# An order edge that keeps lane work behind the weight split of its k-step

## Chip, cores and metric

One core of one Trainium2 chip. The metric is the device time of one execution in microseconds (us); the median of three runs is quoted. A profile of one further execution shows where the time is. Engines are named as in the profile: PE (TensorE matmul), PEld (its weight loads), DVE (VectorE), ACT (ScalarE), POOL (GpSimd), SP (SyncE, whose queue issues the DMAs).

## What is computed

One layer of a bidirectional hybrid encoder for two requests, a sample of 1024 tokens and a prompt of 256, with shared weights and a width of 2048:

```python
hn = rms_norm(x, norm_g)
proj = hn @ w_in
xbc, z_ssd, dt_raw, q, k, v, z_att, mq, z_mem = split_cols(proj, IN_SIZES)
xbc = silu(centred_dwconv(xbc, conv_w, conv_b))          # 5 taps
y = ssd_scan(forward) + ssd_scan(backward) + d_skip * xs # chunks of 128 tokens, 16 heads
o_ssd = rms_norm(y * silu(z_ssd), ssd_norm_g)            # per group of 512
o_att = window_attention(q, k, v, sink) * silu(z_att)    # |t-s| <= 128, 8 heads
o_mem = softmax(mq @ mk.T) @ mv * silu(z_mem)            # 256 memory tokens, 4 heads
return x + concat([o_ssd, o_att, o_mem]) @ w_out
```

All inputs and outputs are float32.

## The kernel before

The 1280 tokens are ten tiles of 128: tiles 0 to 7 are the sample, 8 and 9 the prompt. They are worked in two groups of five tiles (640 tokens). The transposed activations of a group lie in SBUF as a high and a low part, `xH` and `xL`, both fp32r. A product with a weight is three fp32r matmuls: high by high, high by low, low by high.

**Blocks and k-steps.** The dense products are cut into blocks of output columns. `block_tok` (L245 to L277) has tokens on the partitions: for each of 16 k-steps it loads 128 x 512 raw weights (`wraw`, four buffers, L228), splits them in `wsplit` (L216 to L223) and issues 15 matmuls (L269, L270, L271) into five accumulators `acc`. `block_feat` (L279 to L313) has features on the partitions: eight double k-steps, raw weights from L286, matmuls of 320 columns (L304, L305, L306) into four of the five accumulators. In both, the last two k-steps are done together, so that accumulators finish one after the other, and each is evacuated (`evac`) at once.

**The weight split.** `wsplit` makes the high part on ACT (`wh`, L219, or L222 with a gain) and the low part on DVE (`wl`, L220 or L223). `wh` and `wl` have three buffers each (`WB`), so the split of a k-step can be issued as soon as the matmuls of the k-step three before are through. The splits are traced under `tc.high_priority(offset=100)`.

**Lanes.** Everything else is written as generators that yield between steps, and queued in two lanes (L143 to L175). `run` (L945) goes through a block, and after each k-step calls `pump`, which takes as many lane steps as the block's entry in `RATES` says, from the two lanes in turn. `need` steps a lane until a named piece is done. The pieces that the prediction speaks of:

- `x_stats(t)` (L922): four loads `xst` and squares (L928), a sum (L930), and `rsqrt` on POOL (L133, L134); it gives the norm of token tile t. `mem_stats(i)` does so for the memory (L940).
- `vectors` (L1012): eight small loads (L1017) and the exponential of `aneg` (L1024).
- `mk_prep(i)` and `k_prep(t)`: load, square, sum, `rsqrt` on POOL, scaling, transposes on PE.
- `attn(t)` (L559): a head (load q, square L571, sum L573, `rsqrt`, L577, high and low part L585 and L586, transposes L591 into `pq`), then for four head pairs the scores (L607 to L627), a turn (L637 into `ppt`, L638) and the product with v (L648 into `po`). `mem_attn(t)` is the like for the memory; its head ends in transposes L684 into `pmq`.
- `ssd_up(t)` (L758): one SSD chunk. `weights(q)`, four times a tile, loads `rf` (two buffers) and `rb` (three buffers) from `ac_d` (L840), adds the columns' bias in eight ACT instructions (L848), merges the two directions (L849, DVE), takes the exponential (L850, ACT) and multiplies by `cb` (L851, DVE). `diag(g)` reads the results in the matmuls `py` (L858).
- `ssd_down(t)`: the backward state.

Other buffers of the lanes: tag `wa` has five, shared by x_stats, mem_stats, the preps and the heads of both attentions; `wb` four.

**Who sets the order.** A scheduler places every instruction when the program is built. It goes by priority (the order of tracing, less the offset of `high_priority`), takes an instruction of lower priority where those above it aren't ready in its own model of time, and gives a tile a buffer when one is free. The result is a fixed order for each engine; on the chip an engine takes its instructions in that order, and each waits for its inputs. So lane work whose inputs come from a load alone can stand ahead of splits and evacuations that were traced before it. Evacuations are traced with high priority, too (offset 30 in `block_tok`, 100 in `block_feat`). `tc.issue_after(ins)` adds, for each instruction that its block traces on the engine of `ins`, an edge that puts it behind `ins` in that engine's order; it adds no wait for `ins` to finish. The kernel uses it already for the loads of `x_stats` and `mem_stats` (L927 and L939, behind the last load of the activations).

Of the kernel before, what the change touches and what calls it, by code (L numbers as in the profile page):

```python
# [10 lines left out]
F32 = mybir.dt.float32  # L11
# [4 lines left out]
AF = mybir.ActivationFunctionType  # L16
ALU = mybir.AluOpType
# [23 lines left out]
def hymba_encoder_kernel(  # L41
# [6 lines left out]
    V, A, G, T, S = nc.vector, nc.scalar, nc.gpsimd, nc.tensor, nc.sync  # L48
# [99 lines left out]
    def queue(lane, fn, ts):  # L148
        for t in ts:
            lanes[lane].append(((fn.__name__, t), fn(t)))  # L150

    def step(lane):
        name, gen = lane[0]
        try:
            next(gen)
        except StopIteration:
            lane.popleft()
            done.add(name)

    def pump(n):  # L160
        for _ in range(n):
            turn[0] ^= 1
            lane = lanes[turn[0]] or lanes[turn[0] ^ 1]
            if lane:
                step(lane)

    def need(fn, ts):

        for t in ts:
            while (fn.__name__, t) not in done:  # L170
                step(next(x for x in lanes if any(nm == (fn.__name__, t) for nm, _ in x)))
# [44 lines left out]
    def wsplit(raw, h, l, g=None):  # L216

        if g is None:
            A.activation(h, raw, AF.Copy)  # L219
            V.tensor_sub(l, raw, h.bitcast(F32))  # L220
        else:
            A.activation(h, raw, AF.Copy, scale=g)  # L222
            V.scalar_tensor_tensor(out=l, in0=raw, scalar=g, in1=h.bitcast(F32), op0=ALU.mult, op1=ALU.subtract)  # L223

    def w_laid(src, n, gain=None):

# [18 lines left out]
    def block_tok(w, nt, evac, before_last=None):  # L245
# [4 lines left out]
        for k in range(KT):  # L250
            raw = wp.tile([P, 512], F32, tag="wraw", name="wraw", bufs=RB)
            load(k, raw[:, :n])
            with tc.high_priority(offset=HP[2]):
                h = wp.tile([P, 512], F32R, tag="wh", name="wh", bufs=WB)
                l = wp.tile([P, 512], F32R, tag="wl", name="wl", bufs=WB)
                wsplit(raw[:, :n], h[:, :n], l[:, :n], gcol(k))
            hls[k] = h, l
            if k == KT - 2:
                continue
            if k == KT - 1 and before_last is not None:  # L260
                before_last(k)

            for t in range(nt):
                for k_ in ((k - 1, k) if k == KT - 1 else (k,)):
                    q, m = divmod(k_, 4)
                    h, l = hls[k_]
                    sh = cur["H", q][:, m, t * P:(t + 1) * P]
                    sl = cur["L", q][:, m, t * P:(t + 1) * P]
                    T.matmul(ps[t][:, :n], sh, h[:, :n], start=(k_ == 0), stop=False)  # L269
                    T.matmul(ps[t][:, :n], sh, l[:, :n], start=False, stop=False)  # L270
                    T.matmul(ps[t][:, :n], sl, h[:, :n], start=False, stop=(k_ == KT - 1))  # L271
                if k == KT - 1:
                    with tc.high_priority(offset=HP[0]):
                        evac(t, ps[t])
            if k == KT - 1:
                yield k - 1
            yield k  # L277

    def block_feat(name, evac):  # L279
# [4 lines left out]
        for kk in range(KT // 2):  # L284
            raw = wp.tile([P, 512], F32, tag="wraw", name="wraw", bufs=RB)
            S.dma_start(raw, src[kk])  # L286
            with tc.high_priority(offset=HP[2]):
                h = wp.tile([P, 2, 256], F32R, tag="wh", name="wh", bufs=WB)
                l = wp.tile([P, 2, 256], F32R, tag="wl", name="wl", bufs=WB)
                wsplit(raw, h.rearrange("p a c -> p (a c)"), l.rearrange("p a c -> p (a c)"))  # L290
            hls[kk] = h, l
            if kk == KT // 2 - 2:
                continue
            tail = kk == KT // 2 - 1

            for kks in ([(kk - 1, kk)] if tail else [(kk,)]):
                for f in range(2):
                    for k in [2 * x + j for x in kks for j in range(2)]:
                        q, m = divmod(k, 4)
                        sh, sl = [x[:, k % 2, f * P:(f + 1) * P] for x in hls[k // 2]]  # L300
                        for half in range(2):
                            c = slice(half * 320, half * 320 + 320)
                            o = ps[f][half][:, :320]
                            T.matmul(o, sh, cur["H", q][:, m, c], start=(k == 0), stop=False)  # L304
                            T.matmul(o, sh, cur["L", q][:, m, c], start=False, stop=False)  # L305
                            T.matmul(o, sl, cur["H", q][:, m, c], start=False, stop=(k == KT - 1))  # L306
                    if tail and f == 0:
                        with tc.high_priority(offset=HP[1]):
                            evac(0, ps[0])
            for k in range(2 * kks[0], 2 * kk + 2):  # L310
                yield k
# [247 lines left out]
    def attn(t):  # L559
# [93 lines left out]
        for step in range(6):  # L653
            if step < 4:
                scores(step)
                yield
            if step >= 2:
                values(step - 2)
                yield
            if 1 <= step <= 4:  # L660
                turn_(step - 1)
                yield
# [517 lines left out]
```

## Time and profile before

| | |
|---|---|
| median of 3 runs | 1917.64 us (1916.83 to 1919.4) |
| profiled execution | 1925.01 us; its span, first to last instruction, 1923.3 us |
| mean granted TensorE clock | 0.994 |
| ACT L219, wh, 128x512, 384 times | 626 ns each |
| DVE L220, wl, 128x512, 384 times | 688 ns each |
| PE L269, 128x512, 1408 times | 406 ns each, pipelined |
| ACT L848, rf and rb, 160 times each | 390 and 391 ns each |
| DVE L849, 40 times | 757 ns each |
| load of rf, of rb (256 KB) | 3.8 and 4.2 us from issue to landing (median) |
| DMA | 289.40 MB, mean 150 GB/s |

How to read the views: a line of the waits gives the engine and line that waited, what released it, the sum in us, the number of times and the longest. A line of the timeline gives the start and length in us, engine, source line, instruction, output and inputs, and in brackets the idle time of the engine before it and what ended it. A line of the stages gives from and to, then the busy time and instructions of PE, PEld, DVE, ACT and POOL, the granted clock, the DMA share and GB/s. Matmuls are pipelined: each is shown with its whole length, and the next one starts before it ends.

### The profile page before, as it was taken

Reading aid. Unit: us, or ns where it says so; the run is one execution under the profiler, and the core shown is the slowest. Engines: PE = TensorE matmul, PEld = TensorE weight load, DVE = VectorE, ACT = ScalarE, POOL = GpSimd, SP = SyncE. Lnnn points to the kernel's source line nnn. Section 1 sums busy time; section 2 is a strip of 40 time slices with the busy share of each in tenths; the row PEclk is TensorE's granted clock in tenths of the full one; section 3 lists DMA queues with packets and bytes.
Section 4 is the critical chain, followed back from the end, with each engine's and each line's share of the span. In section 5 each row is a group of like instructions: output and inputs, shape, how many; then the busy total and the mean of one; then the engine's idle time right before and its main releaser. Section 6 shows DMA issues by size and latency. Waiting matters only on the chain.

```text
span 1923.3 us, 28675 instructions
## 1 busy us (share of the span) xinstructions
PE 1875.9 (98%) x10568; PEld 1634.2 (85%) x10568; DVE 1049.4 (55%) x2133; ACT 760.9 (40%) x1721; POOL 81.6 (4%) x147
## 2 busy tenths in 40 slices
PE   8999989999999999999999999999999999999999
PEld 6779989998898879999978778978978787778887
DVE  4443646677564555667776554576675454542222
ACT  6462463333452545423436444334453333421121
POOL 1010010000000000000100000000000000000000
PEclk9999999999999999999999999999999999999999
DMA  8683563233343545433444567655555345454432
GB/s 272 198 257 104 157 182 121 85 114 109 116 124 113 154 140 172 138 96 101 140 131 142 158 177 247 209 187 162 170 158 186 123 149 159 136 176 132 133 120 69
DMA packets 191340, 289.40 MB, mean 150 GB/s; under 512 B 18977, under 2 KB 68193, under 8 KB 191201
## 3 DMA queue, kind: packets, MB, share of 16 engines
q1 hardware_dynamic: 191056, 287.53, 48.9%
q8 instruction: 83, 1.36, 0.3%
q14 instruction: 57, 0.46, 0.1%
q10 hardware_dynamic: 144, 0.06, 0.0%
HBM read 230.59 MB, written 56.92 MB: 149 GB/s over the span
## 4 chain that ended last, share of the span: by engine, by line
PE 77%; DMA 11%; ACT 4%; DVE 4%; issue 2%; POOL 1%; SPq 1%; ACTq 0%; DVEq 0%; POOLq 0%
PE acc L269 14%; PE acc L270 14%; PE acc L271 14%; PE acc L304 8%; PE acc L305 8%; PE acc L306 8%; DMA xst<-in_x_sample_dram 2%; DMA rf<-ac 2%; PE po L648 2%; PE py L858 1%; PE ppt L637 1%; DMA rb<-ac 1%; DVE wl L220 1%; PE pst L826 1%; PE pst L817 1%
## 5 line engine op out<-in xcount | busy, mean ns | idle before, releaser
L269 PE MATMUL acc<-wh,xH 128*128 128x512 f32 (+1 forms) x1568 | 619.0, 395 | 9.0 <-ACT wh L219 5.6
L270 PE MATMUL acc<-wl,xH 128*128 128x512 f32 (+1 forms) x1568 | 601.6, 384 | 2.9 <-DVE wl L220 2.7
L271 PE MATMUL acc<-wh,xL 128*128 128x512 f32 (+1 forms) x1568 | 600.3, 383 | 0.0
L220 DVE TENSOR_TENSOR wl<-wraw,wh 128x512 fp32r<-128x512 f32 (+1 forms) x416 | 278.3, 670 | 384.4 <-ACT wh L219 376.1
L219 ACT ACTIVATE wh<-wraw 128x512 fp32r<-128x512 f32 (+1 forms) x416 | 254.1, 612 | 528.7 <-PE acc L271 268.0
L304 PE MATMUL acc<-xH,wh 128*128 128x320 f32 x1280 | 406.1, 317 | 9.0 <-DVE zs L331 4.7
L306 PE MATMUL acc<-xH,wl 128*128 128x320 f32 x1280 | 396.6, 310 | 1.6 <-DVE wl L220 1.4
L305 PE MATMUL acc<-xL,wh 128*128 128x320 f32 x1280 | 396.6, 310 | 0.0
L269 PEld LDWEIGHTS acc<-wh,xH 128*128 128x128 f32 x1568 | 296.4, 189 | 69.2 <-issue 8.4
L270 PEld LDWEIGHTS acc<-wl,xH 128*128 128x128 f32 x1568 | 296.7, 189 | 62.9 <-issue 6.6
L271 PEld LDWEIGHTS acc<-wh,xL 128*128 128x128 f32 x1568 | 296.2, 189 | 56.5 <-issue 0.6
L304 PEld LDWEIGHTS acc<-xH,wh 128*128 128x128 f32 x1280 | 241.3, 189 | 15.0 <-DVE zs L331 5.2
L305 PEld LDWEIGHTS acc<-xL,wh 128*128 128x128 f32 x1280 | 241.3, 189 | 3.3 <-issue 3.2
L306 PEld LDWEIGHTS acc<-xH,wl 128*128 128x128 f32 x1280 | 241.1, 188 | 2.3 <-DVE wl L220 2.3
L223 DVE SCALAR_TENSOR_TENSOR wl<-wraw,vec,wh 128x512 fp32r<-128x512 f32 x64 | 48.0, 750 | 128.0 <-ACT wh L222 128.0
L222 ACT ACTIVATE wh<-wraw,vec 128x512 fp32r<-128x512 f32 x64 | 46.3, 723 | 145.4 <-PE acc L271 132.3
L379 DVE SCALAR_TENSOR_TENSOR c<-u,vec,c 128x638 f32<-128x638 f32 (+1 forms) x96 | 84.5, 880 | 1.0
L848 ACT ACTIVATE rb<-rb,wj_all 128x128 f32<-128x128 f32 x160 | 53.0, 391 | 49.1 <-DMA rb<-ac 46.5
L848 ACT ACTIVATE rf<-rf,wj_all 128x128 f32<-128x128 f32 x160 | 53.6, 390 | 33.5 <-DMA rf<-ac 33.5
L622 ACT ACTIVATE lg<-lg,nm 128x384 f32<-128x384 f32 (+1 forms) x80 | 45.1, 564 | 46.2 <-DVE nm L616 46.1
L849 DVE COPY_PREDICATED rb<-upper,rf 128x512 f32<-128x512 uint32 x40 | 30.3, 757 | 53.0 <-ACT rb L848 52.8
L214 DVE SCALAR_TENSOR_TENSOR xL<-chd,vec,xH 128x640 fp32r<-128x640 f32 (+1 forms) x48 | 39.6, 837 | 23.5 <-ACT xH L213 23.5
(238 smaller groups left out, 1725.5 us busy)
## 6 DMA issues: line engine op xcount, KB each, us to landing
wraw<-in_w_in_laid_dram SPq DMA_DIRECT2D x288, 256.0 KB, 2.8
wraw<-in_w_out_laid_dram SPq DMA_DIRECT2D x128, 256.0 KB, 2.7
chd<-in_x_turned_dram SPq DMA_DIRECT2D x32, 320.0 KB, 4.1
rf<-ac SPq DMA_DIRECT2D x40, 256.0 KB, 3.8
rb<-ac SPq DMA_DIRECT2D x40, 256.0 KB, 4.2
out_dram<-yt SPq DMA_DIRECT2D x40, 256.0 KB, 3.6
wraw<-in_w_mem_laid_dram SPq DMA_DIRECT2D x32, 256.0 KB, 4.3
xst<-in_x_sample_dram SPq DMA_DIRECT2D x32, 256.0 KB, 4.9
```

What stands on the lines that cost most here:

```text
L219: A.activation(h, raw, AF.Copy)
L220: V.tensor_sub(l, raw, h.bitcast(F32))
L222: A.activation(h, raw, AF.Copy, scale=g)
L223: V.scalar_tensor_tensor(out=l, in0=raw, scalar=g, in1=h.bitcast(F32), op0=ALU.mult, op1=ALU.subtract)
L269: T.matmul(ps[t][:, :n], sh, h[:, :n], start=(k_ == 0), stop=False)
L270: T.matmul(ps[t][:, :n], sh, l[:, :n], start=False, stop=False)
L271: T.matmul(ps[t][:, :n], sl, h[:, :n], start=False, stop=(k_ == KT - 1))
L304: T.matmul(o, sh, cur["H", q][:, m, c], start=(k == 0), stop=False)
L305: T.matmul(o, sh, cur["L", q][:, m, c], start=False, stop=False)
L306: T.matmul(o, sl, cur["H", q][:, m, c], start=False, stop=(k == KT - 1))
L379: V.scalar_tensor_tensor(out=c[:, :n], in0=u[:, k:k + n], scalar=cw[k], in1=c[:, :n], op0=ALU.mult, op1=ALU.add)
L848: A.activation(r[:, c], r[:, c], AF.Identity, bias=wj_all[:, t, h:h + 1])
```

## The change

`wsplit` keeps its two instructions in a list, `marks`, which always holds those of the last split traced. `step` now takes a lane step inside one `issue_after` for each of them. With that, every ACT instruction of the step stands behind the ACT half of the last traced split in ACT's order, and every DVE instruction behind the DVE half in DVE's order. That split is the one of the k-step after which the step is pumped (in the last two k-steps of a block, the block's last). Instructions of PE, POOL and SP, the loads among them, get no edge. The evacuations, the refills of the activations and `x_rows(1)`, which is not taken through `step`, get none.

```diff
+    marks = []
+
     def step(lane):
         name, gen = lane[0]
         try:
-            next(gen)
+
+            with ExitStack() as st:
+                for ins in marks:
+                    st.enter_context(tc.issue_after(ins))
+                next(gen)
         except StopIteration:
             lane.popleft()
             done.add(name)
...
         if g is None:
-            A.activation(h, raw, AF.Copy)
-            V.tensor_sub(l, raw, h.bitcast(F32))
+            a = A.activation(h, raw, AF.Copy)
+            b = V.tensor_sub(l, raw, h.bitcast(F32))
         else:
-            A.activation(h, raw, AF.Copy, scale=g)
-            V.scalar_tensor_tensor(out=l, in0=raw, scalar=g, in1=h.bitcast(F32), op0=ALU.mult, op1=ALU.subtract)
+            a = A.activation(h, raw, AF.Copy, scale=g)
+            b = V.scalar_tensor_tensor(out=l, in0=raw, scalar=g, in1=h.bitcast(F32), op0=ALU.mult,
+                                       op1=ALU.subtract)
+        marks[:] = a.ins, b.ins
```

## The prediction

> **What bounds the kernel now.** I read the busy shares first, then the start times of PE's matmuls, then what DVE and ACT did ahead of each PE gap, and last the clock.
>
> From the page's first part:
>
> ```profile
> PE 1875.9 (98%) x10568; PEld 1634.2 (85%) x10568; DVE 1049.4 (55%) x2133; ACT 760.9 (40%) x1721; POOL 81.6 (4%) x147
> ```
>
> PE is busy all the time, DVE and ACT about half. In an undisturbed stretch the 512-column matmuls start every 0.227 us and the 320-column ones every 0.147 us, so I laid every PE start in the timeline against that pace. Gaps of over 0.45 us beyond it: 28, together 41.2 us. That is nearly all that an order of instructions can win. It can lose more.
>
> The largest gap is at a block's end. Timeline of DVE (start, length, instruction, idle before it):
>
> ```profile
> 253.70 0.88 DVE L331 TENSOR_TENSOR zs<-acc,rbc 128x320 f32<-128x320 f32 x2
> 256.72 0.73 DVE L849 COPY_PREDICATED rb<-upper,rf 128x512 f32<-128x512 uint32 x1 [2.14 <-ACT rb L848]
> 258.36 0.69 DVE L220 TENSOR_TENSOR wl<-wraw,wh 128x512 fp32r<-128x512 f32 x1
> 259.94 0.29 DVE L471 TENSOR_TENSOR kr<-kr,krr 128x128 f32<-128x128 f32 x1 [0.89 <-POOL krr L134]
> 260.15 0.88 DVE L331 TENSOR_TENSOR zs<-acc,rbc 128x320 f32<-128x320 f32 x2
> ```
>
> and of PE:
>
> ```profile
> 260.69 0.63 PE L304 MATMUL acc<-xH,wh 128*128 128x320 f32 x1 [4.43 <-DVE zs L331]
> ```
>
> PE waits for the second L331, which frees an accumulator. Ahead of it in DVE's queue stand L849 of `ssd_up(0)`, whose result PE reads at 516, and L471 of `k_prep(3)`; both sit out their inputs, and all behind them waits. ACT does the same on lane loads:
>
> ```profile
> ACT rb L848 <- DMA rb<-ac: 46.5, 23, 4.8
> ACT rf L848 <- DMA rf<-ac: 33.5, 23, 4.3
> ACT xst L928 <- DMA xst<-in_x_sample_dram: 15.6, 13, 3.8
> ```
>
> A gap costs more than its length. Stages of the span (PE busy, then the others, the clock, the DMA share):
>
> ```profile
> 57.94:64.77 6.83, 6.14 (x14) 4.81 (x15) 1.98 (x3) 2.75 (x5) 0.00 (x0) 0.50 0.62 189
> 64.77:71.60 6.83, 6.83 (x32) 5.64 (x30) 1.68 (x3) 2.43 (x4) 0.00 (x0) 1.00 0.28 84
> 259.33:266.15 6.82, 5.46 (x22) 5.42 (x23) 4.15 (x11) 4.85 (x14) 0.58 (x1) 0.50 0.81 257
> 1402.79:1406.20 3.41, 3.41 (x14) 2.82 (x14) 2.13 (x5) 0.60 (x1) 0.00 (x0) 0.50 0.91 320
> 1631.48:1634.90 3.42, 3.42 (x10) 2.65 (x9) 0.69 (x1) 0.57 (x1) 0.00 (x0) 0.50 0.79 268
> ```
>
> The granted clock is 0.50 for 6.8 us after the gaps of 3.54 (at 58.6) and 4.60 us (at 260.7), and for 3.4 us after those of 1.54 (at 1401.2) and 2.80 us (at 1630.8). Against the usual pace that lost a further 3.0, 2.4, 1.6 and 1.6 us.
>
> **The change, part by part.** It adds no instruction. The edge goes to ACT's and DVE's work of a step; the step's DMAs (SP) and its `rsqrt` (POOL) get none.
>
> *What moves.* I followed the source's queues and numbered each step with the split it is issued with, then laid that beside the order in which ACT and DVE ran. Today 408 of 861 lane operations on ACT (178 us of work) and 197 of 1148 on DVE (109 us) run ahead of that split. 315 and 93 of them are `ssd_up`'s, its weights (L848 to L850) by 9 to 332 us; the rest is `x_stats`, `k_prep`, `mk_prep` and `attn`'s head. The others trail their split already, mostly by three splits, because PE hands them their input.
>
> *What it removes.* Gaps that a moved operation made, clock loss included:
> - 254 to 266: 0.45 + 4.60 + 2.4 = 7.5 us. `ssd_up` and `k_prep(3)` go; `x_stats(6)` belongs to splits issued just there and may stay. I take 6.
> - 137 to 148: 0.62 + 1.20 + 1.15 = 3.0. DVE's splits stood behind `mk_prep`, which waits 1.4 us for POOL three times; it belongs to splits of 167 and later. I take 3.
> - 285 and 295: 0.61 + 1.98, by `attn(0)`'s head and `x_stats(8, 9)`, due at 320 to 340. I take 2.6.
> - 935 and 1511: 1.08 + 1.67, by `k_prep(6, 7)` and `attn(9)`'s head. I take 2.5.
> - 58.6: 3.5 + 3.0. ACT sat 5.0 us before `vectors`' aneg L1024 with an evacuation L411 behind it; but that evacuation also needed the store mq<-mkr, which SP issued at 53.3 behind eight small loads (L1017) and which landed at 57.9. Those loads don't move. Ends 0 and 6.5, I take 2.
> - 771, 1146, 1192, 1216, 1389, 1401, 1423: 10.9 us, where moved weights on ACT or DVE were one cause of several. Ends 0 and 10.9, I take 4.
>
> Sum 20; at most 33.
>
> *What it adds.* A lane operation now waits behind a split, and that waits for PE to free wh: up to 5.5 us at a time (ACT wh L219 on PE acc L271, 268 us in all). Queued behind it on ACT are other lane work and evacuations; behind those DVE, and PE's next lane step. For `ssd_up`'s weights I cost that at nothing: eight L848 of 0.39, L849 0.76, L850 0.63, L851 0.68 make some 5.2 us with the overlap of starts, and from today's split to the first py L858 that reads them there are 13.0 us (tile 6) to 44 us. The cover is two or three k-steps of matmuls (15 x 0.227 = 3.4 us each). Without it each py waits as at 1171 (1.10 us). For the rest I pushed every moved operation to its split and on along its data: no PE instruction came late; the nearest have 5.3 us left (`mk_prep`), 9.4 (`attn`), 9.6 (`k_prep`).
>
> *Buffers.* Loads keep their early start but hold their buffers (rf 2, rb 3, wa 5) until the split. In the densest place, tile 5, the splits of the first and third weights end at 1058.0 and 1062.3: rf is free at about 1062.5, reloaded (3.8 us) by 1066.5, and the weights done by 1072; py reads them at 1084.7. SP waits in order for that buffer, and raw weights stand behind; four raw buffers cover it.
>
> *New gaps.* The moved work takes its waits for POOL and neighbours along. Today it costs PE about 16 us (the first four points); at the new places 0 if the loads have long landed and no evacuation stands behind, 16 if it is as bad there. I take 8, the middle, since the loads' waits go and the POOL waits stay.
>
> Net: 8 - 20 = -12 us. The profiled execution took 1925.0 us (span 1923.3), 7.4 more than the median of 1917.6; it would take 1913, and the median 1906.
>
> **Two rules weighed.** Row: the clock halved after gaps of 1.54 and 2.80 us. The Trainium skill (TensorE: Matmul & The Clock Gate, "HAM oscillation") puts the limit at idle of some 3.4 us; this trace does not bear that limit out. By the page the 1.6 us of clock in the last point would be no gain, and the net an estimated -11.
>
> Row: at 1630.8 PE waited for `mem_attn(8)`'s head, which doesn't run early today. The Trainium skill (Perfetto Trace Analysis, "Optimization Strategy") advises to make what the busy engine waits for start sooner. By that advice an edge that starts lane work later is a step the wrong way; the third case below prices this from rows.
>
> **The rivals.**
> 1. *Given back:* evacuations now meet the same lane work at other block ends, new gaps of 16 to 24 us. For it: 287 us of work only changes its place. Against: its loads will have landed. Time 1914 to 1921.
> 2. *No effect:* the order hardly changes. Against it: 605 operations must move. I count it into the first.
> 3. *Slower:* heads of attention tiles (load, L571, L573, POOL 1.65 us, L577, L585) lose their lead, and PE stands at the transposes. The price is in the timeline of PE:
>
> ```profile
> 1630.79 0.63 PE L684 MATMUL pmq<-ident,mq 128*128 128x128 f32 x4 [2.64 <-issue]
> ```
>
> 2.8 us and 1.6 of clock, 4.4 a head; it decides from five heads on (22 against 20). Eight of the ten `attn` heads would give 35 - 20 = +15, so 1933. For it: `mem_attn(8, 9)`, with no lead, do wait. Against: there three steps lay within about one k-step; `attn`'s heads keep 9.4 us.
>
> **How the numbers follow.** Forecast 0.63, given back 0.11, slower 0.26. A change of 0.2% (3.8 us) is about what a measurement of this kernel can tell. Predicted is 1906. Low end: all 33 us gained less 8, 1893. High end: just short of the third case, 1931. The forecast's own range is 1893 to 1913.
>
> **What would show it.** Right: no gap at 255 to 261 and 137 to 148, L848 of `ssd_up(0)` no earlier than about 480, ACT's waits for rf, rb and xst loads down from 107 us to under 70, PE gaps of over 0.45 us nearer 25 than 41 us. Wrong: gaps of PE at pq L591, ppt L637 or py L858, or more half-clock stages than these four.

## The result and the profile after

The kernel after takes 1896.99 us (median of 4 runs, 1895.86 to 1898.42), beside 1918.52 us for the kernel before on the same chip (4 runs, 1916.83 to 1923.84): ratio 0.9871, 95% interval 0.985 to 0.9891. That is 21.5 us less; forecast were 12 less. The profiled executions are 1925.01 and 1896.01 us, 29.0 apart, so some 7 us of that difference belong to the one execution before and not to the kernels. A second profile of the kernel before (below) has its gaps in the same places and somewhat shorter.

All of the difference lies between PE's matmuls. Laid against the usual pace as in the prediction, PE's starts are late by 55.3 us in all before and by 26.4 after, 28.9 less. Gaps of over 0.45 us went from 28 (41.2 us) to 15 (18.3 us); half-clock time from 20.5 us in four stages to 10.2 in two.

The first part of the page after, busy times by engine:

```profile
PE 1868.3 (99%) x10568; PEld 1631.4 (86%) x10568; DVE 1053.4 (56%) x2133; ACT 758.3 (40%) x1721; POOL 80.6 (4%) x147
```

The counts are those of before: nothing was added, only placed differently. (Lines behind the edit are numbered 6 to 8 higher than before: the split is L225 and L226, the 512-column matmul L277, the accumulator's L331 is L339, the weights L848 to L851 are L856 to L859, py is L866.)

DVE's timeline after, at the block's end where before it stood idle 2.14 us for ACT's rb and 0.89 for POOL's krr, with L331 behind them:

```profile
240.21 0.83 DVE L341 SCALAR_TENSOR_TENSOR zs<-th,zs 128x640 f32<-128x640 f32 x1 [0.81 <-ACT th L340]
241.24 0.69 DVE L226 TENSOR_TENSOR wl<-wraw,wh 128x512 fp32r<-128x512 f32 x1 [0.20 <-ACT wh L225]
241.99 0.93 DVE L339 TENSOR_TENSOR zs<-acc,rbc 128x320 f32<-128x320 f32 x2
243.00 0.69 DVE L226 TENSOR_TENSOR wl<-wraw,wh 128x512 fp32r<-128x512 f32 x1
...
248.56 0.29 DVE L479 TENSOR_TENSOR kr<-kr,krr 128x128 f32<-128x128 f32 x1 [1.08 <-POOL krr L134]
```

Both L339 now run in one go between two splits, with no lane work ahead of them, and PE has no gap there. The wait for POOL is no shorter (1.08 us, before 0.89), but it falls at 248.6, after the evacuation, and PE has no gap there either. `ssd_up(0)`'s first L856 starts at 463.1, where before it was 237.7.

ACT's waits for its lane loads (releaser, sum in us, times, longest), which came to 46.5, 33.5 and 15.6 on these lines before:

```profile
ACT rb L856 <- DMA rb<-ac: 24.3, 8, 5.3
ACT xst L936 <- DMA xst<-in_x_sample_dram: 10.2, 8, 3.9
ACT rf L856 <- DMA rf<-ac: 2.0, 3, 1.0
```

What PE waits for after:

```profile
PE acc L277 <- ACT wh L225: 5.4, 1, 5.4
PE pr L202 <- DVE ch L199: 4.0, 4, 1.5
PE pmq L692 <- issue: 3.4, 2, 2.2
PE ppt L645 <- DVE lg L635: 2.6, 2, 1.4
PE acc L277 <- DVE zs L329: 1.8, 1, 1.8
PE pcb L783 <- DMA bc<-xbc_d: 1.4, 1, 1.4
```

The first is the start of the kernel (5.4 us until the first split). Of the two waits at `ppt`, the longer one falls at 377 and is new. DVE's timeline ahead of it:

```profile
375.28 0.75 DVE L585 SCALAR_TENSOR_TENSOR q<-q,rx,qr 128x512 f32<-128x512 f32 x1 [1.77 <-POOL qr L134]
...
376.62 0.61 DVE L635 TENSOR_SCALAR lg<-lg,den 128x256 f32<-128x256 f32 x2
```

L585 belongs to the head of the next attention tile. It waits 1.77 us for POOL ahead of L635, the last step before the transposes for which PE stands.

Evacuations behind lane work (`zs L331`, 4.7 us before) have left the list but for `zs L329`, a new one. Its place in DVE's timeline:

```profile
1092.60 0.68 DVE L859 TENSOR_TENSOR rb<-rb,cb 128x512 f32<-128x512 f32 x1
1093.96 0.69 DVE L329 SCALAR_TENSOR_TENSOR zs<-th,acc 128x512 f32<-128x512 f32 x1 [0.69 <-DMA z<-zs]
...
1096.77 0.69 DVE L329 SCALAR_TENSOR_TENSOR zs<-th,acc 128x512 f32<-128x512 f32 x1 [1.52 <-DMA z<-zs]
```

The evacuation L329 waits for the store of an earlier zs to give back its buffer, in a stretch where tile 5's weights are now made (L859). That store took 4.58 us from issue to landing (1092.10 to 1096.68), right behind a load of `rf` that SP issued at 1091.54. With the edge on all steps but `ssd_up`'s (below), no such load stands there, the same store was issued at 1092.03 and landed after 2.69 us, and PE has no gap. PE loses 2.01 us here, and the clock halves behind it (stages: PE, PEld, DVE, ACT, POOL busy, granted clock, DMA share, GB/s):

```profile
1091.50:1098.33 6.83, 4.91 (x21) 3.42 (x20) 4.62 (x9) 4.68 (x10) 0.00 (x0) 1.00 0.65 213
1098.33:1105.16 6.83, 6.83 (x26) 6.06 (x25) 2.82 (x5) 1.56 (x4) 0.00 (x0) 0.50 0.71 218
1603.50:1606.92 3.42, 3.42 (x12) 2.75 (x11) 0.67 (x1) 0.50 (x1) 0.00 (x0) 0.50 0.83 288
```

The second stage costs a further 3.3 us against the pace. The third follows the 2.38 us that PE stands at `mem_attn(8)`'s head (`pmq L692 <- issue` above), which stood there before too (2.80).

### The profile page after: what moved, and what is told of

It is laid out like the page before. It is cut to its first block, busy times and chain, and to the rows that moved or that the text cites. A ratio compares the mean times of both kernels' runs of the same rounds, so it can differ in the third digit from the quotient of the medians.

```text
span 1893.9 us, 28656 instructions
## 1 busy us (share of the span) xinstructions
PE 1868.3 (99%) x10568; PEld 1631.4 (86%) x10568; DVE 1053.4 (56%) x2133; ACT 758.3 (40%) x1721; POOL 80.6 (4%) x147
## 4 chain that ended last, share of the span: by engine, by line
PE 92%; DMA 4%; DVE 1%; ACT 1%; issue 1%; POOL 0%; SPq 0%; ACTq 0%; DVEq 0%
PE acc L277 17%; PE acc L278 17%; PE acc L279 17%; PE acc L312 10%; PE acc L314 10%; PE acc L313 10%; PE po L656 2%; PE py L866 2%; PE ppt L645 1%; PE pmo L743 1%; PE pyb L914 1%; PE pyf L820 1%; DMA ch<-o 1%; PE psc L615 1%; PE pst L825 1%
## 5 line engine op out<-in xcount | busy, mean ns | idle before, releaser
L277 PE MATMUL acc<-wh,xH 128*128 128x512 f32 (+1 forms) x1568 | 618.0, 394 | 7.6 <-ACT wh L225 5.4
L226 DVE TENSOR_TENSOR wl<-wraw,wh 128x512 fp32r<-128x512 f32 (+1 forms) x416 | 278.5, 670 | 398.5 <-ACT wh L225 359.9
L225 ACT ACTIVATE wh<-wraw 128x512 fp32r<-128x512 f32 (+1 forms) x416 | 255.3, 614 | 599.2 <-PE acc L279 286.3
L277 PEld LDWEIGHTS acc<-wh,xH 128*128 128x128 f32 x1568 | 295.6, 189 | 68.2 <-issue 8.0
L856 ACT ACTIVATE rb<-rb,wj_all 128x128 f32<-128x128 f32 x160 | 52.9, 390 | 24.3 <-DMA rb<-ac 24.3
L856 ACT ACTIVATE rf<-rf,wj_all 128x128 f32<-128x128 f32 x160 | 51.6, 390 | 2.0 <-DMA rf<-ac 2.0
L219 ACT ACTIVATE xH<-chd,vec 128x640 fp32r<-128x640 f32 (+1 forms) x48 | 37.3, 790 | 30.5 <-DMA chd<-in_x_turned_dram 10.1
```

Of the source, the lines that this page charges most:

```text
L225: a = A.activation(h, raw, AF.Copy)
L226: b = V.tensor_sub(l, raw, h.bitcast(F32))
L856: A.activation(r[:, c], r[:, c], AF.Identity, bias=wj_all[:, t, h:h + 1])
```

## Experiments

Three theories went in. **Theory 1**: each gap is made by particular lane work that stands ahead of an evacuation or a split, and goes when that work stands behind. **Theory 2**: splits get ahead of lane work in general, so that the gain goes with the number of operations held back. **Theory 3**: any new order of the queues shifts gaps, and this one fell well by luck. Every ratio is to the kernel before, run beside it on the same chip (its medians: 1913.51 us for the first four experiments, 1911.68 for the next four, 1916.8 for the last four).

### Only `ssd_up`'s steps get the edge

```diff
-                for ins in marks:
+                for ins in marks if name[0] == 'ssd_up' else ():
```

> The edges are kept for the steps of ssd_up alone (315 of the 408 ACT and 93 of the 197 DVE operations that the change moves). Theory 1 (each PE gap was made by particular lane work that stood, with its inputs not yet there, ahead of an evacuation or a split; removing that work removes that gap): the gap at 260 (4.6 us and its clock loss) loses its longest cause, L849, and shrinks to 0 to 2.5 us, the gaps from 771 to 1423 go (about 9 of 10.9 us), while 58.6, 137 to 148, 285, 295, 935 and 1511 stay (15.8 us with clock); time 10 to 14 us under before, ratio about 0.994. Theory 2 (the splits themselves come sooner, whatever lane work is moved; ssd_up has two thirds of it): two thirds of the 21.5 us, so 14 us, with the gaps thinned everywhere alike. Theory 3 (any new order falls a per cent up or down, the gaps have no one cause): no relation of gaps to the work moved, time anywhere from -25 to +15 us.

1906.26 us, ratio 0.9962 (0.9949 to 0.9976): 7.3 us less, under what was expected. 22 gaps with 27.3 us stay. What PE waits for:

```profile
PE acc L277 <- ACT mkr L419: 3.3, 1, 3.3
PE acc L312 <- DVE u L371: 2.7, 1, 2.7
PE acc L278 <- DVE wl L226: 2.3, 4, 1.0
PE acc L312 <- DVE zs L339: 1.8, 1, 1.8
```

`zs L339`, the 260 gap, is 1.8 us instead of 4.4: `ssd_up(0)` has gone from ahead of it, `k_prep(3)` and `x_stats(6)` have not. The gap at 58, the pair at 140 and 145 and the one at 289 stay.

### All steps but `ssd_up`'s get it

```diff
-                for ins in marks:
+                for ins in marks if name[0] != 'ssd_up' else ():
```

> The edges are kept for all lane steps but ssd_up's. Theory 1: the gaps at 58.6, 137 to 148, 285, 295, 935 and 1511 go (15.8 us with clock), that at 260 stays in part (L849 still stands there), those from 771 to 1423 stay; time 13 to 18 us under before, ratio about 0.992; the gains of this run and of the one with ssd_up alone add up to the whole, 21.5 us. Theory 2: a third of the whole, 7 us. Theory 3: anywhere, and the two don't add up.

1892.62 us, ratio 0.9887 (0.9871 to 0.9903): 20.9 us less, about the whole change's effect. All of the early gaps are gone but for 0.53 us at 54 and 0.69 at 245, and there is none near 1097. Of those from 771 to 1423, which were expected to stay, several are there (1.96 at 1122, 1.31 at 1375). Its waits:

```profile
ACT rb L856 <- DMA rb<-ac: 44.9, 25, 5.1
ACT rf L856 <- DMA rf<-ac: 31.2, 24, 7.3
```

ACT still waits 76 us for `ssd_up`'s loads, as before the change, and the kernel is fast. So those waits cost little once the other lane work is held back, and theory 2 falls: 408 of the 605 operations that had run ahead of their split are `ssd_up`'s, and holding them alone gave 7.3 us; holding the other 197 gave 20.9. Theory 1 had expected the two parts to add up, and they do not: 28.2 is more than the whole's 21.5. Both parts take a share of the 260 gap, and `ssd_up`'s edges bring the new gap at 1097 (it is at 1110, 1.54 us, with them alone).

### Only ACT's edge, only DVE's

```diff
-        marks[:] = a.ins, b.ins
+        marks[:] = a.ins,
```

> Edges for the lanes' ACT operations alone. Most moved DVE operations read what a moved ACT operation writes and would follow by data, but the scheduler places them by its own clock. Theory 1: all but the gaps made by DVE work with no ACT ahead of it goes; 17 to 21.5 us under before. Theory 2: the ACT half of the split comes first in its chain, so as much as the whole change. Theory 3: anywhere.

1893.54 us, ratio 0.989 (0.9874 to 0.9906): 20.0 us less.

```diff
-        marks[:] = a.ins, b.ins
+        marks[:] = b.ins,
```

> Edges for the lanes' DVE operations alone; ACT may run lane work ahead as before, and sits before loads (xst, mkr, aneg, rf, rb) as before, about 100 us in sum. Theory 1: DVE's queue is clear at 255 to 260 (L849 and L471 no longer ahead of L331) and at 137 to 148, so those 10 us go; ACT's share stays (58.6, 295 and part of the rest); 8 to 14 us under before. Theory 2: little, since the ACT half of each split is still late; 0 to 6 us. Theory 3: anywhere.

1900.02 us, ratio 0.9925 (0.9912 to 0.9939): 13.5 us less. The gap at 57 is the one early gap that DVE's edge leaves, at 2.27 us and with 3.4 us of half clock; those of 137 to 148 and 255 to 261 are gone under either edge. Lane steps go from ACT to DVE and back, so that holding one half holds much of the other. The traces show it. Take the longest sequence that two kernels' orders share and count what falls out of it: against the kernel before, that is 283 of DVE's 2133 instructions with both edges and 244 with ACT's alone, 394 of ACT's 1721 with both and 240 with DVE's alone. The intervals of ACT's edge alone and of the whole change overlap.

### The edge goes to the split of two k-steps earlier

```diff
+    hist = []
...
-        marks[:] = a.ins, b.ins
+        hist.append((a.ins, b.ins))
+        marks[:] = hist[max(0, len(hist) - 3)]
```

> The changed kernel with looser edges: a lane step stands behind the split two k-steps before its own. Of the moved operations nearly all ran three splits or more ahead, so they still move. Theory 1 (the gaps were made by lane work far ahead of its place with inputs not there): as the changed kernel within 0.4%, 18 to 24 us under before, and the gaps at 58, 137 to 148, 255 to 261, 285, 295 gone. Theory 2 (it is the splits' being first that pays): a part is lost, since splits can again stand behind lane work of two k-steps; 8 to 16 us under before. Theory 3 (any new order falls a per cent up or down): anywhere, with other gaps.

1892.23 us, ratio 0.9892 (0.9871 to 0.9913): 19.4 us less. A looser edge does as well. The lane work only must not run ahead by a whole block; how closely it follows the split decides nothing. 15 gaps with 18.7 us, as in the kernel after, at partly other places (1.37 at 56, 1.15 at 452, 1.52 at 1481; none at 1097).

### A control: another order without edges

The kernel before, with the weight splits traced at a priority offset of 90 instead of 100:

```diff
-HP = (30, 100, 100)
+HP = (30, 100, 90)
```

> A control: the kernel before, with no edges, and the splits' priority offset 90 in place of 100, which makes the scheduler place the program anew but leaves lane work free to run ahead. Theory 1: lane work still stands ahead (ssd_up's first L848 near 238 us), gaps of over 0.45 us keep a sum of 30 to 50 us, time within 8 us of before. Theory 2: the splits come a little later, 0 to 6 us over before. Theory 3: a change of 10 to 25 us up or down, as large as that of the change.

1915.02 us, ratio 1.001 (0.9996 to 1.0024). What PE waits for:

```profile
PE acc L304 <- DVE zs L331: 5.5, 1, 5.5
PE acc L269 <- ACT mkr L411: 3.2, 1, 3.2
PE acc L306 <- DVE wl L220: 2.2, 2, 1.6
```

The large gaps are those of the kernel before: 5.61 at 260, 3.31 at 59, the group from 137 to 146; one of 1.77 at 427 is new. As a test of theory 3 this is weak, since the order is nearly the old one: by the same count only 25 of ACT's instructions and 84 of DVE's left it, where the change moved 394 and 283. More weighs that `ssd_up`'s edges alone moved 320 and 188 and left the gaps of the other lane work standing, while four ways of holding that work back lost the same gaps.

### Only `vectors` gets the edge

```diff
-                for ins in marks:
+                for ins in marks if name[0] == 'vectors' else ():
```

> Edges for the steps of vectors alone (one ACT and three DVE operations). It asks what made the gap at 58.6 (3.5 us, with 3.0 of clock). If it was ACT sitting before aneg: the gap is gone. If it was the store mq<-mkr, which SP issued behind the small loads (which keep their place): a gap of 2 to 3.5 us stays near 58. All other gaps as before.

1910.38 us (one execution). PE's waits:

```profile
PE acc L312 <- DVE zs L339: 4.7, 1, 4.7
PE acc L277 <- ACT mkr L419: 1.9, 1, 1.9
```

The gap at 56 stays at 2.09 us with aneg out of the way, so aneg was not its main cause. In the kernel after, ACT's timeline has the evacuation itself waiting for the store, the wait that PE shares no longer:

```profile
53.07 0.60 ACT L419 ACTIVATE mkr<-acc 128x512 f32<-128x512 f32 x1 [3.73 <-DMA mq<-mkr]
```

SP issued that store at 49.2, before at 53.3, in both cases behind five of the eight small loads (of the others one is issued at 16, two at 70 or later): 43.8 to 48.0 after, 48.0 to 52.7 before, where one of them held SP for 2.05 us instead of 0.33. Some other step's ACT edge must have drawn these loads forward: the gap is gone or under 0.6 us with the edge on ACT alone and with the edge on all but `ssd_up`, and stays with the edge on DVE alone.

The traces point to `mem_stats`. In the kernel before, its squares stand ahead of splits and wait for their loads:

```profile
42.52 0.63 ACT L940 ACTIVATE mst<-mst 128x512 f32<-128x512 f32 x1 [1.91 <-DMA mst<-in_mem_prompt_dram]
49.34 0.63 ACT L940 ACTIVATE mst<-mst 128x512 f32<-128x512 f32 x1 [1.92 <-DMA mst<-in_mem_prompt_dram]
```

Between 30 and 52 us ACT waits 5.9 to 6.4 us for these loads of the prompt's memory in each of the six profiles with a gap of 2.09 to 3.54 us, 3.2 us in the experiment with the split of two k-steps earlier, where the gap is 1.37, and not at all in the seven others, where it is under 1 us. A raw weight load of SP stands until 44.5 for the split behind the first of these squares, and the small loads and the store follow it. An edge for `mem_stats` alone was not tried.

### The heads of the last two memory tiles first

With the kernel after, 2.4 and 1.4 us of gap stay at pmq, where `mem_attn(8)` and `mem_attn(9)` come right behind `mem_swap`. Here the first step of each (load of mq, its norm) is queued ahead of `mem_swap`; all edges are kept:

```diff
-    queue(0, mem_swap, [0])
-    queue(0, mem_attn, range(8, 10))
+    late = {t: mem_attn(t) for t in (8, 9)}
+
+    def heads(_):
+        for t in (8, 9):
+            next(late[t])
+            yield
+
+    queue(0, heads, [0])
+    queue(0, mem_swap, [0])
+    for t in (8, 9):
+        lanes[0].append((("mem_attn", t), late[t]))
```

> The changed kernel, with the first step (load, square, sum, norm, scale) of mem_attn(8) and mem_attn(9) queued before mem_swap, where it stood behind it and behind mem_attn(8). After the change PE still waits 2.4 and 1.4 us at their transposes (L692, at 1602 and 1623), with 1.6 us of halved clock after the first. Theory 1: both gaps and the half-clock stage go, 3 to 5.4 us under the changed kernel. Against it: the next wait in the same chain (the refill of the last activations behind mem_attn(9), 1.6 and 1.2 us at 1653 and 1674) takes it back; 0 to 2 us.

1886.71 us, ratio 0.9862 (0.9839 to 0.9885). Both pmq gaps are gone.

### The best ones side by side

The kernel after, that with the heads first, the same with the edge for all but `ssd_up`, and the kernel before once more with a profile:

> The changed kernel once more, beside the next two on one chip. Ratio to before 0.985 to 0.990; the gap at 1097 (2.0 us) with its half-clock stage, and those at 1602 and 1623, are there again.

> The changed kernel with the heads of mem_attn(8) and mem_attn(9) queued before mem_swap, beside the changed kernel on one chip. Theory 1: the two gaps and the half-clock stage (5.4 us) are gone from its end, so 3 to 6 us under the changed kernel. Against it: 0 to 2 us, if the refill of the last activations waits the longer.

> The heads queued before mem_swap, and edges for all lane steps but ssd_up's. With edges for the rest alone no gap showed near 1097 (2.0 us and 3.0 of clock in the changed kernel, where an evacuation waits with its store behind pinned weights), but 1.6 us at 1122 and 1.3 at 1375 stayed. Theory 1: the two about cancel, within 3 us of the run with the heads alone. If the edges for ssd_up were worth what they are worth alone (7 us): 7 us slower than that run.

> The kernel before once more, for a second profile: the executions of it on this chip lay between 1908 and 1920 us, the first profiled one at 1925. Theory 1: the gaps at 58, 137 to 148, 255 to 261, 285 to 295 and 1400 to 1423 are there in both, and the difference is in their lengths and in the number of half-clock stages. Theory 3: the gaps are elsewhere.

After: 1894.59 us, ratio 0.9887 (0.9872 to 0.9902). Heads first: 1884.37 us, ratio 0.9837 (0.9822 to 0.9852), 10.2 us under the kernel after and the fastest of all. Heads first without `ssd_up`'s edges: 1888.91 us, ratio 0.9862 (0.9847 to 0.9876); that is 4.5 us more, between the 3 and the 7 us of its expectation. The intervals of the two ratios just overlap, but the five executions of the one (1883.38 to 1887.66) all lie below the four of the other (1888.44 to 1892.14). With the heads first, `ssd_up`'s edges thus seem worth having; without, the two kernels were not told apart (0.9871 and 0.9887, on different chips). The kernel before: 1914.39 us.

Stages of the kernel after, then of the one with heads first, over the places of pmq and of the transposes pr that follow:

```profile
1597.60:1604.00 6.40, 5.60 (x25) 4.77 (x26) 2.39 (x4) 1.23 (x2) 0.00 (x0) 0.73 0.86 285
1649.00:1657.00 8.00, 6.65 (x21) 5.30 (x22) 3.81 (x8) 1.19 (x2) 0.00 (x0) 0.57 0.49 159
```

```profile
1590.00:1597.00 7.00, 7.00 (x34) 5.83 (x33) 4.39 (x8) 3.07 (x6) 1.21 (x2) 1.00 0.92 276
1640.00:1648.00 8.00, 7.59 (x41) 6.06 (x41) 6.10 (x12) 3.70 (x7) 0.00 (x0) 1.00 0.65 186
```

The expectation of 3 to 6 us counted the two pmq gaps (3.8 us) and a stage of clock. Between the two profiles lie 12.0 us: 3.8 at pmq, 2.7 at pr (the gaps there went from 4.2 to 1.5 us), and most of the other 5.5, as far as can be argued, is 13.7 us of half clock that the second one lacks.

PE's waits in the second profile of the kernel before:

```profile
PE acc L304 <- DVE zs L331: 4.7, 1, 4.7
PE acc L269 <- ACT mkr L411: 2.4, 1, 2.4
```

Its gaps stand where they stood in the first one (2.55 at 57, the pair at 139 and 144, 4.83 at 257, 1.98 at 291), 34.8 us in all beside 41.2, and PE's starts are 45.0 us late beside 55.3. The gaps belong to the order, their exact lengths to the execution. Against this profile the kernel after has 18.6 us less, against the first 28.9; the 21.5 of the medians lie between.

## Why the prediction was right, and where it was off

The forecast, faster because the gaps that lane work makes are lost, came out; the measured time lies in its own range (1893 to 1913), 9 us below its value. The terms it took for gains, 20 us in all, came to 30.6 against the first profile of the kernel before (7.5, 3.0, 2.6, 2.75, 6.5 and 8.3) and to some 22.5 against the second, where the same gaps are shorter (7.0, 2.3, 2.0, 2.2, 4.1 and 4.9). By its own steps:

- **The bound.** Right: the gain is in PE's gaps, 28.9 of 29.0 us between the profiles.
- **254 to 266, 137 to 148, 285 and 295, 935 and 1511**: taken 6, 3, 2.6 and 2.5 us. All went, whole. Reserving 1.5 us for `x_stats(6)` was wrong; it made no gap. That the first has two causes is shown: with `ssd_up` alone held back the 260 gap is 1.9 us, with only the other steps held back it is gone, 0.69 being left at 245.
- **58.6**: taken 2 between ends of 0 and 6.5; it was the whole (6.5, and 4.1 by the second profile). This term was mis-sized the most: it held SP's loads for fixed, because they get no edge (and counted eight ahead of the store, where there are five). They did not move in SP's order past the store, but the whole group ran some 4 us sooner, and the store with it; the traces point to `mem_stats`, which the term did not have. An edge on one engine moved when another engine's queue got through.
- **771 to 1423**: taken 4 of 10.9; 8.3 went (0.78, 1.31 and 0.54 stay; 4.9 by the second profile). Too small as well: moved work that was named as one cause of several was mostly the one that decided.
- **Outside the list**: some 5 us more by the first profile (0.98 at 470, 1.56 at 668, about 1 of the 2.57 at 984, several of half a microsecond or less), 2 to 3 by the second. The sum had nothing for them; their causes were not tried.
- **New gaps**: taken 8, the middle of 0 and 16. Measured: 1.39 at 377, 0.63 at 961, 0.55 more at 1002, 2.01 and 3.3 us of clock at 1097, together 7.9. That the sizes agree is luck. The reason given, waits for POOL that go along, holds for 1.39 us: L585 at 377, ahead of L635; the wait at 248.6 cost PE nothing. Two thirds came from a store's buffer at 1097, in `ssd_up`'s dense tile 5, which the term did not have; and at 1002 a wait of ACT for a load of `rb`, ahead of attention's exponentials, was not lost but grew (4.76 to 5.32 us).
- **`ssd_up`'s weights at nothing**: right at the reader. PE's waits at py do not grow (gaps of 0.83 and 0.54 beside 1.10 and 1.54). The price fell on the evacuation's buffer instead, at 1097.
- **The third case, heads losing their lead**: PE has no wait at pq. The `ppt L645 <- DVE lg L635` at 377, 1.39 us in each kernel with edges on `attn` and absent without them, is not of this kind: the head that waits for POOL there is done 9.4 us before its own transposes. Nearest to it is the 0.63 us at 961, where `k_prep`'s transposes L492 wait for `kh` L484. It needed five heads at 4.4 us.
- **The clock rule.** The Trainium skill (TensorE: Matmul & The Clock Gate, "HAM oscillation") puts the limit at some 3.4 us of idle. The runs bear out the row rather than the page: half clock came after gaps of 1.49 (heads first, at 1097) and 2.01 us (after, at 1097). To count the clock as a gain was right for the large gaps; for a gap of 1.5 us it is a matter of the execution, as the last section shows.
- **The advice to start sooner** (the Trainium skill, Perfetto Trace Analysis, "Optimization Strategy") was weighed as speaking against this change. For the heads at pmq it holds (10.2 us with the gaps behind them). Against the change it did not speak: what PE waited for at 260 was the evacuation, and that starts sooner because `k_prep` and `ssd_up` start later.
- **Signs.** Gaps at 255 to 261 and 137 to 148 gone, 463 for the first weight of `ssd_up(0)` where 480 was named as the earliest, gaps at 18.3 us, two half-clock stages: as forecast, but 17 us earlier at the weight. ACT's waits for loads fell to 38 us as named, but the sign was empty: without `ssd_up`'s edges they stay near 76 us on rf and rb alone, and the time is about the same (ratios 0.9887 and 0.9871).

## What to carry to other kernels

Where a busy engine is fed by two others whose queues run in order, look at each of its gaps for what stands *ahead* of the feeder in the feeder's queue: work that is not due for 100 us can stop a block's end, and starting it later is the gain. It need not be placed closely (two k-steps of slack did as well), and the long waits it had are no measure of what it cost; the wait that ends last at the busy engine is. An edge moves the waits of the queues that it does not touch, so a term that rests on "this queue doesn't move" needs its far end in the sum.

## What the runs showed of the hardware

Half clock does not follow from the length of the one gap ahead of it. It came after 1.49 us (heads first, at 1097) and 1.55 us (after, second profile, at 1095), and not after 2.33 us (heads first without `ssd_up`'s edges, at 1366) or 2.16 us (ACT's edge only, at 1095). Nor does its length: 3.4 us after a gap of 3.28 (all but `ssd_up`, at 1601), 6.8 after one of 2.01 (after, at 1098). The kernel after had 10.2 us of it in one execution and 13.7 in another, the kernel before 20.5 and 13.7. Most stages last 3.4 us or twice that.
